# Heads of a bidirectional gated linear attention layer: log-decay sums moved to the first stage, states carried by VectorE with two factors in one operation, sums of squares written by ScalarE

## The chip, the core and the metric

The kernel runs on one core of one Trainium2 chip. Five engines work side by side, each through its own list of instructions in order: TensorE (PE, its weight loads PEld), VectorE (DVE), ScalarE (ACT), GpSimd (POOL) and SyncE (SP), which issues most of the DMA transfers. An instruction whose input is not ready holds up everything behind it on its engine. The metric is the device time of one launch in microseconds (us).

## The reference

One layer with two attention branches over a sequence of T = 1024 positions and a width of 1024. GLA has 4 heads (keys of 128, values of 256), HGRN 8 heads (keys of 128, values of 128). Each head runs a gated linear attention forwards and backwards in chunks of 64:

```
p = x @ W_in
g = log_sigmoid(low_rank(p)) / 16                       # GLA: log decay, <= 0
g = log(lb + (1 - lb) * sigmoid(p_f)),  k = 1 - exp(g)  # HGRN
b = cumsum(g) within a chunk of 64
o = (q * exp(b)) @ S  +  scores(q, k, exp(b_i - b_j)) @ v
S = exp(b_last) * S + (k * exp(b_last - b))^T @ v
o = forward + backward;  o * rsqrt(mean(o*o) + 1e-6) * gain * silu(gate);  then @ W_branch
y = sigmoid(m_a) * y_gla + sigmoid(m_h) * y_hgrn;  out = layer_norm(alpha * x + y @ W_out)
```

## The kernel before

**Three stages.** `dense` (0 to some 715 us of the profiled execution) makes all projections of x; every float32 product is done as three products of float32 numbers split into a high and a low part (`split`, L91 on ACT and L92 on DVE), with seven products in place of eight (`seven`). `heads` (about 715 to 1213 us) does the attention of the 12 heads and, between them, products that do not depend on them (`merge_gate`, later `gla_branch`; tile `proj`, L1364). The last stage (`hgrn_branch`, `final`) merges the branches, multiplies by W_out and normalises. Between stages everything passes through DRAM tensors: `logs` holds the log decays, `ks`, `qs`, `vd` and `gated` keys, queries, values and gates.

**Order.** The order on each engine is made by the framework's scheduler, which places instructions when the program is built, by priorities (raised in `high_priority` blocks) and by its own costs. On the chip the lists are fixed. A tile name has a fixed number of buffers; a new tile takes a buffer when the last reader of the old one is done.

**Log decays in `dense`.** `narrow_job` of kind decay (8 jobs, two directions of one HGRN head each) makes four 128x512 tiles `h`, from which POOL makes the keys (L1200) and ACT, in place, the logarithm (L1202); POOL's queue stores them to `logs`. `gla_logs` (8 calls, one for a head and a direction) works in two of five `raw` buffers of 128x1024, `f` and `m`: Abs, Exp and Ln on ACT (L1168 to L1171), the minimum and the difference on DVE (L1169, L1172), then a store. The same five `raw` buffers take the weights that are loaded for the next products.

**A head in `heads`.** `decays` loads the log decays into FB and FF. `scaled` sums them on DVE with a scan along 1024 columns that starts anew every 64 (L1422; `runs` is 1, and 0 at the starts), into PB and PF. It takes the ends of the halves (`logs`, `ends`), subtracts the middle (L1437), makes exp(-b) and exp(b) on ACT (L1440, L1441) and multiplies by keys and queries on DVE (L1443, L1442). `scores` makes the masked scores A (PE L382; DVE L392, L393, L395); `transposed` turns the keys (PE L540, ACT L541). PSUM tiles `sc`, `st`, `po` and `proj` have two buffers each.

**The states** (`states`) run once backwards (into Sb) and once forwards (into Sf), 7 steps each, over chunks of 128 positions. PE makes the products `st` (4 chunks in one PSUM tile for HGRN, 2 for GLA). ACT multiplies each by the decay of the near half into V (L1566), DVE adds the old state times the decay of the whole chunk (L1568, `tot`), and ACT multiplies by the decay of the next chunk's far half into Sb or Sf (L1572), which PE reads in the product `po` (L566).

**The norm** in `attend`: ACT squares a `po` tile of 128x512 (L1525), DVE adds up in groups of dv columns (L1526) and scales (L1528), POOL takes the power -1/2 (L1529), DVE multiplies by it and by the gate (L1533). PE transposes the result (L1540), ACT multiplies by the gain (`ot`, L1546), SP stores it to `oa` or `oh`. `gla_rows` loads `oa` back for the GLA branch product (tile `x`).

Of the kernel before, what the change touches and what calls it, by code (L numbers as in the profile page):

```python
# [12 lines left out]
AF = mybir.ActivationFunctionType  # L13
ALU = mybir.AluOpType
AX = mybir.AxisListType

P = 128
# [3 lines left out]
NT = T // P  # L21
# [853 lines left out]
class Fast(Layer):  # L875
# [283 lines left out]
    def gla_logs(self, h, d):  # L1159

        nc = self.nc
        f, m = self.t("raw"), self.t("raw")
        bias = self.prm[:, 4 * d + h : 4 * d + h + 1]
        for n in range(2):
            o = slice(512 * n, 512 * n + 512)
            ps = self.bank()
            nc.tensor.matmul(ps, self.ups[:, d, P * h : P * h + P], self.lr[:, o], start=True, stop=True)
            nc.scalar.activation(f[:, o], ps, AF.Abs, bias=bias)  # L1168
            nc.vector.tensor_scalar(out=m[:, o], in0=ps, scalar1=bias, scalar2=0.0, op0=ALU.add, op1=ALU.min)  # L1169
        nc.scalar.activation(f, f, AF.Exp, scale=-1.0)  # L1170
        nc.scalar.activation(f, f, AF.Ln, bias=1.0)  # L1171
        nc.vector.tensor_tensor(out=f, in0=m, in1=f, op=ALU.subtract)  # L1172
        self.store(self.logs[2 * h + d], f)

    def narrow_job(self, kind, at, w):
        nc = self.nc
        late = []

        def out(i, j, _, c, psum):
            s = c if kind == "copy" and not psum else self.h()  # L1180
            col = slice(512 * j, 512 * j + 512)
            if kind == "scale":
                nc.scalar.mul(s, c, QSCALE)
            elif kind != "copy":
                nc.scalar.activation(s, c, AF.Sigmoid)
            elif psum:
                nc.scalar.copy(s, c)
            if kind == "swish":
                nc.vector.scalar_tensor_tensor(out=s, in0=c, scalar=QSCALE, in1=s, op0=ALU.mult, op1=ALU.mult)
            if kind == "decay":  # L1190
                late.append((i, col, s))
            else:
                self.store((self.ks if kind == "copy" else self.qs)[at + i][:, col], s)

        self.seven(self.narrow_product(w, self.xs), 1, out, at == 0 and kind == "decay")
        for i, col, s in late:
            n = HGRN_HEADS * i + at
            o, b = self.omlb[:, n : n + 1], self.lb[:, n : n + 1]
            k = self.h()
            nc.gpsimd.tensor_scalar(out=k, in0=s, scalar1=self.nomlb[:, n : n + 1], scalar2=o, op0=ALU.mult, op1=ALU.add)  # L1200
            self.store(self.ks[GLA_HEADS + n][:, col], k)
            nc.scalar.activation(s, s, AF.Ln, scale=o, bias=b)  # L1202
            self.store(self.logs[2 * (GLA_HEADS + at) + i][:, col], s)

    def wide_job(self, kind, columns, w):
# [18 lines left out]
    def dense(self):  # L1224
        nc = self.nc
        self.slot, self.stage_one = T, True
        self.counts = {"raw": 5, "s": 3, "w": 8, "h": 14}
        heads = GLA_HEADS + HGRN_HEADS
        self.qs = self.dr.tile([heads, P, T], F32, name="qs")
        self.ks = self.dr.tile([GLA_HEADS + 2 * HGRN_HEADS, P, T], F32, name="ks")  # L1230
# [164 lines left out]

    def decays(self, n):

        fs = []
        for d in (1, 0):
            f = self.t("FB" if d else "FF")  # L1400
            self.nc.sync.dma_start(out=f, in_=self.logs[2 * n + d])
            fs.insert(0, f)
        return fs

    def key(self, n):
        k = self.t("K")
# [5 lines left out]
        self.nc.sync.dma_start(out=q, in_=self.qs[n])  # L1412
        return q

    def scaled(self, q, k, f, unit, d, index):

        nc = self.nc
        pr = self.t("PB" if d else "PF")
        last = 0 if d else 63
        seg = lambda a: a.rearrange("p (s j) -> p s j", j=64)  # L1420
        step = -1 if d else 1
        nc.vector.tensor_tensor_scan(  # L1422
            out=pr[:, ::step],
            data0=self.runs,
            data1=f[:, ::step],
            initial=0.0,
            op0=ALU.mult,
            op1=ALU.add,
        )
        logs = self.t(f"logs{d}", (P, NT, 2))  # L1430
        ends = self.t(f"ends{d}", (P, NT, 2))
        flat = lambda a: a.rearrange("p c h -> p (c h)")
        nc.vector.tensor_copy(out=flat(logs), in_=seg(pr)[:, :, last])
        nc.vector.tensor_reduce(out=self.minp[:, index : index + 1], in_=flat(logs), axis=AX.X, op=ALU.min)
        nc.scalar.activation(flat(ends), flat(logs), AF.Exp, scale=unit)
        half = pr.rearrange("p (c h j) -> p c h j", h=2, j=64)[:, :, d, :]
        nc.vector.tensor_tensor(  # L1437
            out=half, in0=half, in1=logs[:, :, d].unsqueeze(2).to_broadcast([P, NT, 64]), op=ALU.subtract
        )
        nc.scalar.activation(f, pr, AF.Exp, scale=-unit)  # L1440
        nc.scalar.activation(pr, pr, AF.Exp, scale=unit)  # L1441
        nc.vector.tensor_tensor(out=pr, in0=pr, in1=q, op=ALU.mult)  # L1442
        nc.vector.tensor_tensor(out=f, in0=f, in1=k, op=ALU.mult)  # L1443
        return pr, f, ends
# [26 lines left out]
    def heads(self):  # L1471
        nc = self.nc
        self.oa = self.dr.tile([KC, P, T], F32, name="oa")
        self.oh = self.dr.tile([KC, P, T], F32, name="oh")
        self.ua = self.dr.tile([KC, P, T], F32, name="ua")
        self.runs = self.t("runs")
        nc.vector.memset(self.runs, 1.0)
        nc.vector.memset(self.runs.rearrange("p (s j) -> p s j", j=64)[:, :, 0], 0.0)
        for n, name in enumerate(self.SEQUENCE):
            (self.gla_front if name[0] == "A" else self.hgrn_front)(int(name[1]))  # L1480
            if n == 0:
                self.plain_x()
            if n in (6, 8):
                self.gla_rows((n - 6) // 2)
            for i in self.MERGES[n]:
                self.merge_gate(i)
            if n >= 8:
                for i in (2 * n, 2 * n + 1):
                    self.gla_branch(i - 16)

    def attend(self, head, prepared, v, ve, dv, gate, gains, row):
        nc = self.nc
# [4 lines left out]
        per = 512 // dv  # L1497
# [11 lines left out]
        ss = self.t("ss", (P, NT), bufs=2)  # L1509
        rs = self.t("rs", (P, NT), bufs=2)  # L1510
        for g in range(NT // per):
            next(chain, None)
            po = self.att_ps("po")
            for j in range(per):
                c = per * g + j
                s = slice(P * c, P * c + P)
# [5 lines left out]
                self.product(po[:, dv * j : dv * j + dv], terms)  # L1522
            cs = slice(per * g, per * g + per)
            sq = self.t("sq", (P, 512))
            nc.scalar.activation(sq, po, AF.Square)  # L1525
            nc.vector.tensor_reduce(out=ss[:, cs], in_=sq.rearrange("p (c e) -> p c e", e=dv), axis=AX.X, op=ALU.add)  # L1526
            ms = self.msall[:, NT * head + per * g : NT * head + per * g + per]
            nc.vector.tensor_scalar(out=ms, in0=ss[:, cs], scalar1=1.0 / dv, scalar2=RMS_EPS, op0=ALU.mult, op1=ALU.add)  # L1528
            nc.gpsimd.tensor_tensor(out=rs[:, cs], in0=ms, in1=self.mhalf[:, cs], op=ALU.pow)  # L1529
            for j in range(per):  # L1530
                c = per * g + j
                gt = gate[:, c, ve : ve + dv]
                nc.vector.scalar_tensor_tensor(  # L1533
                    out=gt, in0=po[:, dv * j : dv * j + dv], scalar=rs[:, c : c + 1], in1=gt, op0=ALU.mult, op1=ALU.mult
                )
# [12 lines left out]

    def states(self, order, kt, v, ve, dv, ends, out_of, way):

        nc = self.nc
        per = 512 // dv
        near, far = (1, 0) if way == 1 else (0, 1)
        tot = self.t(f"tot{way}", (P, NT), bufs=2)
        nc.vector.tensor_tensor(out=tot, in0=ends[:, :, 0], in1=ends[:, :, 1], op=ALU.mult)
        order = list(order)
        state = None
        for b in range(0, len(order), per):
            pu = self.att_ps("st")
            batch = order[b : b + per]  # L1560
            us = [pu[:, dv * i : dv * i + dv] for i in range(len(batch))]
            for u, c in zip(us, batch):
                self.product(u, [(kt[:, P * c : P * c + P], v[:, c, ve : ve + dv])])
            for n, (u, c) in enumerate(zip(us, batch), b):
                new = self.t("V", (P, 256), bufs=6)[:, 0:dv]
                nc.scalar.mul(new, u, ends[:, c, near : near + 1])  # L1566
                if n:
                    nc.vector.scalar_tensor_tensor(  # L1568
                        out=new, in0=state, scalar=tot[:, c : c + 1], in1=new, op0=ALU.mult, op1=ALU.add
                    )  # L1570
                state = new
                nc.scalar.mul(out_of(n, c), state, ends[:, c + way, far : far + 1])  # L1572
            yield

    def judge(self):
# [116 lines left out]
    def run(self):  # L1692
        of = lambda *names: [f"{name}{k}" for name in names for k in range(4)]
        with ExitStack() as ctx:
# [3 lines left out]
            with ExitStack() as kept:  # L1698
                self.keep_x = self.pool(kept, "keepx")
                with ExitStack() as c:  # L1700
                    self.tops = self.pool(c, "tops")
                    self.stage(c, "p0", [["raw"], ["s"], ["w"], ["h"]])
                    self.dense()
                with ExitStack() as c:
                    self.stage(
# [6 lines left out]
                            ["Sf", "sq"],  # L1712
                            ["V"],
                            ["FB", "FF"],
                            ["runs"],
                            ["PB", "PF"],
                            ["v"],
                            ["A", "KT", "Sb"],
# [92 lines left out]
```

## Time and profile before

| | us |
|---|---|
| median of 3 runs | 1425.37 (1425.27 to 1426.08) |
| the profiled execution | 1426.49 |
| its span, from the first to the last record | 1424.80 |
| granted TensorE clock, mean of the span | 0.975 |

[...]

### The profile page before, as it was taken

The numbers are of one execution on the slowest core, as the hardware profiler recorded it, in microseconds if no ns is written. First come the engines' busy times: TensorE is split into PE (matmuls) and PEld (weight loads), VectorE is DVE, ScalarE is ACT, GpSimd is POOL, SyncE is SP. The second block draws the span as 40 slices with busy tenths as digits, with TensorE's granted clock in tenths as the row PEclk, the third lists the DMA queues.
The fourth block names the chain that finished last, engine by engine and source line by source line (L and its number), as shares of the span: only waits on it lengthen the run. The fifth ranks groups of instructions, "written<-read, shape, count | busy, mean of one in ns | idle before, by whom it ended". The sixth has DMA issues, their size and how long they took to land.

```text
span 1424.8 us, 21066 instructions
## 1 busy us (share of the span) xinstructions
PE 1339.6 (94%) x8009; PEld 1152.1 (81%) x8009; DVE 862.4 (61%) x1410; ACT 670.6 (47%) x1190; POOL 182.9 (13%) x270
## 2 busy tenths in 40 slices
PE   7999979999999999999989999987889999799996
PEld 5888858877799999999968877765677888577885
DVE  8755645776566665544463666766788443665544
ACT  6656565774533333222244565556676454653100
POOL 1234350111111011011100010111110100000011
PEclk9999989999999999999999999998899999899998
DMA  7444342333433332332473454355565331865431
GB/s 274 140 148 167 129 151 101 135 138 111 154 131 108 107 102 99 99 114 104 144 278 121 139 185 166 109 177 177 178 231 212 104 112 60 294 231 169 150 103 55
DMA packets 83153, 210.45 MB, mean 148 GB/s; under 512 B 10656, under 2 KB 10656, under 8 KB 80992
## 3 DMA queue, kind: packets, MB, share of 16 engines
q1 hardware_dynamic: 68368, 160.48, 33.1%
q0 software_dynamic: 14672, 48.51, 9.0%
q8 instruction: 65, 1.06, 0.3%
q14 instruction: 48, 0.39, 0.1%
HBM read 137.65 MB, written 71.30 MB: 147 GB/s over the span
## 4 chain that ended last, share of the span: by engine, by line
PE 71%; DMA 10%; DVE 7%; ACT 5%; issue 5%; POOL 0%; SPq 0%; DVEq 0%; POOLq 0%; ACTq 0%
PE bank L988 22%; PE bank L975 16%; PE proj L1364 12%; PE bank L1636 6%; PE po L566 4%; PE st L566 3%; DMA raw<-in_dram 3%; PE sc L382 2%; DMA wraw<-in_dram 2%; PE bank L1304 2%; DMA g<-ua 2%; DMA oa<-ot 1%; PE sc L540 1%; DVE PF L1422 1%; DMA hraw<-oa 1%
## 5 line engine op out<-in xcount | busy, mean ns | idle before, releaser
L975 PE MATMUL bank<-xP,w 128*128 128x512 f32 x1344 | 315.5, 395 | 13.6 <-DVE h L1012 7.0
L988 PEld LDWEIGHTS bank<-w,xP 128*128 128x128 f32 x2688 | 323.5, 192 | 1.1 <-DVE w L92 0.8
L988 PE MATMUL bank<-w,xP 128*128 128x256 f32 x2688 | 323.6, 283 | 0.3 <-DVE w L92 0.3
L975 PEld LDWEIGHTS bank<-xP,w 128*128 128x128 f32 x1344 | 255.1, 190 | 71.4 <-DVE h L1012 8.4
L1364 PE MATMUL proj<-x,hw 128*128 128x512 f32 x576 | 147.1, 399 | 0.1
L92 DVE TENSOR_TENSOR w<-s,w 128x512 fp32r<-128x512 f32 (+1 forms) x96 | 84.0, 877 | 76.3 <-ACT w L91 76.1
L91 ACT CAST w<-s 128x512 fp32r<-128x512 f32 (+1 forms) x96 | 72.6, 760 | 121.7 <-PE bank L988 78.7
L91 ACT CAST w<-raw 128x512 fp32r<-128x512 f32 (+1 forms) x90 | 65.1, 732 | 128.4 <-PE bank L988 67.0
L1364 PEld LDWEIGHTS proj<-x,hw 128*128 128x128 f32 x576 | 104.9, 188 | 21.9 <-issue 0.7
L1364 PE MATMUL proj<-xP,hw 128*128 128x512 f32 x360 | 97.8, 411 | 6.3 <-DVE hw L92 5.5
L1364 PE MATMUL bank<-oh,hw 128*128 128x512 f32 x384 | 93.1, 401 | 9.9 <-ACT hw L91 4.8
L1529 POOL TENSOR_TENSOR rs<-msall,mhalf 128x4 f32<-128x4 f32 (+1 forms) x32 | 43.0, 1343 | 447.2 <-DVE msall L1528 444.5
L1364 PEld LDWEIGHTS bank<-oh,hw 128*128 128x128 f32 x384 | 72.4, 192 | 30.5 <-ACT hw L91 7.9
L1012 DVE TENSOR_TENSOR h<-bank,h 128x512 f32<-128x512 f32 x96 | 65.8, 687 | 45.9 <-PE bank L988 33.4
L92 DVE TENSOR_TENSOR w<-raw,w 128x512 fp32r<-128x512 f32 (+1 forms) x90 | 75.3, 843 | 29.6 <-ACT w L91 29.6
L1364 PEld LDWEIGHTS proj<-xP,hw 128*128 128x128 f32 x360 | 67.2, 193 | 21.9 <-DVE hw L92 6.6
L1012 DVE TENSOR_TENSOR h<-h,bank 128x512 f32<-128x512 f32 x65 | 44.4, 684 | 53.9 <-PE bank L988 28.7
L92 DVE TENSOR_TENSOR hw<-hraw,hw 128x512 fp32r<-128x512 f32 x64 | 43.8, 687 | 42.5 <-ACT hw L91 42.5
L1566 ACT ACTIVATE V<-st,ends 128x128 f32<-128x128 f32 (+1 forms) x168 | 58.6, 414 | 22.5 <-PE st L566 22.2
L566 PE MATMUL st<-v,KT 128*128 128x128 f32 (+1 forms) x336 | 61.0, 323 | 2.6 <-ACT KT L541 1.4
L1304 PE MATMUL bank<-xP,w 128*128 128x512 f32 x216 | 52.3, 404 | 8.0 <-ACT xP L91 6.6
L91 ACT CAST hw<-hraw 128x512 fp32r<-128x512 f32 x64 | 39.6, 618 | 36.9 <-PE proj L1364 25.6
(194 smaller groups left out, 2008.2 us busy)
## 6 DMA issues: line engine op xcount, KB each, us to landing
raw<-in_dram SPq DMA_DIRECT2D x82, 256.0 KB, 3.2
hraw<-in_dram SPq DMA_DIRECT2D x68, 256.0 KB, 3.5
raw<-in_dram SPq DMA_DIRECT2D x33, 512.0 KB, 3.7
ks<-h POOLq DMA_DIRECT2D x40, 256.0 KB, 3.1
K<-ks SPq DMA_DIRECT2D x20, 512.0 KB, 4.9
logs<-h POOLq DMA_DIRECT2D x32, 256.0 KB, 3.7
gated<-h POOLq DMA_DIRECT2D x32, 256.0 KB, 2.7
vd<-h POOLq DMA_DIRECT2D x32, 256.0 KB, 2.7
```

The costliest lines, as they stand in the source:

```text
L91: nc.scalar.copy(hi, raw)
L92: (lo_engine or nc.gpsimd).tensor_tensor(out=lo, in0=raw, in1=hi.bitcast(F32), op=ALU.subtract)
L382: mm = lambda out, l, r: nc.tensor.matmul(out, l, r, start=True, stop=True)
L566: self.nc.tensor.matmul(out, l, r, start=(i == 0), stop=(i == len(terms) - 1))
L975: self.nc.tensor.matmul(out[0], a[i][:, k, :], b[k][:, j, :], start=(n == 0 and not more), stop=(n == len(terms) - 1), skip_group_check=True,)
L988: self.nc.tensor.matmul(out[c // 2][:, 256 * (c % 2) : 256 * (c % 2) + 256], b[k][:, j, P * c : P * c + P], a[i][:, k, :], start=(n == 0 a ...
L1012: nc.vector.tensor_tensor(out=to[n], in0=one[n], in1=two[n], op=op)
L1304: self.nc.tensor.matmul(ps, w.both[a][:, k, :], xs[k][:, b, :], start=(m == 0), stop=(m == len(terms) - 1))
L1364: nc.tensor.matmul(ps, parts[k][a], self.plain[k, n][:, b, :], start=(m == 0), stop=(m == len(terms) - 1))
L1529: nc.gpsimd.tensor_tensor(out=rs[:, cs], in0=ms, in1=self.mhalf[:, cs], op=ALU.pow)
L1566: nc.scalar.mul(new, u, ends[:, c, near : near + 1])
L1636: nc.tensor.matmul(pss[m], y[:, k, rows], self.wo[k, n][:, j, part], start=(i == 0), stop=(i == len(terms) - 1))
```

## The change

Four things change.

- **Sums in `dense`.** The scan moves from `scaled` to `sum_up`, which runs in place on a log-decay tile before it is stored, in pieces of 512 columns with `runs` of that width. There are 32 pieces in the decay jobs and 16 in `gla_logs`. To make room for `runs`, `h` has 13 buffers and no longer 14. In `heads` the loads of `logs` go into PB and PF, and FB and FF are only written by ACT. In GLA the store of `f` and in HGRN that of `h` now wait for DVE.
- **States by DVE.** Both multiplications of a step become one DVE operation with two factors (`tensor_scalar`), and the sum with the old state comes before it: `total = entered + u`, `entered = total * near * far`. ACT's 336 multiplications and `tot` go. The products `st` stay in PSUM until DVE's chain has come to them.
- **Sums of squares.** ACT squares in pieces of dv columns (96 in all) with an accumulator output for the sum; the 32 reductions on DVE go.
- **Buffers.** `runs` leaves the second stage.

```diff
         nc.vector.tensor_tensor(out=f, in0=m, in1=f, op=ALU.subtract)
+        self.sum_up(f, d)
         self.store(self.logs[2 * h + d], f)
+
+    def sum_up(self, f, d):
+
+        for n in range(f.shape[1] // 512):
+            u = f[:, 512 * n : 512 * n + 512][:, :: -1 if d else 1]
+            self.nc.vector.tensor_tensor_scan(out=u, data0=self.runs, data1=u, initial=0.0, op0=ALU.mult, op1=ALU.add)
...
             nc.scalar.activation(s, s, AF.Ln, scale=o, bias=b)
+            self.sum_up(s, i)
             self.store(self.logs[2 * (GLA_HEADS + at) + i][:, col], s)
...
-        self.counts = {"raw": 5, "s": 3, "w": 8, "h": 14}
+        self.runs = self.t("runs", (P, 512))
+        nc.vector.memset(self.runs, 1.0)
+        nc.vector.memset(self.runs.rearrange("p (s j) -> p s j", j=64)[:, :, 0], 0.0)
+        self.counts = {"raw": 5, "s": 3, "w": 8, "h": 13}
...
-            f = self.t("FB" if d else "FF")
-            self.nc.sync.dma_start(out=f, in_=self.logs[2 * n + d])
+            pr = self.t("PB" if d else "PF")
+            self.nc.sync.dma_start(out=pr, in_=self.logs[2 * n + d])
...
-        pr = self.t("PB" if d else "PF")
+        f = self.t("FB" if d else "FF")
...
-        nc.vector.tensor_tensor_scan(
...
-            nc.scalar.activation(sq, po, AF.Square)
-            nc.vector.tensor_reduce(out=ss[:, cs], in_=sq.rearrange("p (c e) -> p c e", e=dv), axis=AX.X, op=ALU.add)
+            for j in range(per):
+                o, c = slice(dv * j, dv * j + dv), per * g + j
+                nc.scalar.activation(sq[:, o], po[:, o], AF.Square, accum_out=ss[:, c : c + 1])
...
-                new = self.t("V", (P, 256), bufs=6)[:, 0:dv]
-                nc.scalar.mul(new, u, ends[:, c, near : near + 1])
                 if n:
-                    nc.vector.scalar_tensor_tensor(
-                        out=new, in0=state, scalar=tot[:, c : c + 1], in1=new, op0=ALU.mult, op1=ALU.add
-                    )
-                state = new
-                nc.scalar.mul(out_of(n, c), state, ends[:, c + way, far : far + 1])
+                    total = self.t("V", (P, 256), bufs=6)[:, 0:dv]
+                    nc.vector.tensor_tensor(out=total, in0=entered, in1=u, op=ALU.add)
+                    u = total
+                entered = out_of(n, c)
+                nc.vector.tensor_scalar(
+                    out=entered,
+                    in0=u,
+                    scalar1=ends[:, c, near : near + 1],
+                    scalar2=ends[:, c + way, far : far + 1],
+                    op0=ALU.mult,
+                    op1=ALU.mult,
+                )
```

What this does to the lists of instructions is shown at three places. In the rows a number behind x counts equal instructions in a row; a scan is printed as SCALAR_TENSOR_TENSOR with `runs` among its inputs; lines of the changed kernel are numbered by its own text.

DVE in `dense`, in the second of the decay jobs: `w` are split weights of the next job, `s` their sums, L1012 adds a product from PSUM (`bank`) into `h`.

```order
@@ -108,4 +114,5 @@
 L92 TENSOR_TENSOR w<-raw,w 128x512
 L1012 TENSOR_TENSOR h<-bank,h 128x512
+L1180 SCALAR_TENSOR_TENSOR h<-runs,h 128x512 x4
 L92 TENSOR_TENSOR w<-s,w 128x512
 L953 TENSOR_TENSOR s<-raw,s 128x512
```

The four scans of a job stand in one piece, ahead of the next split.

DVE in `heads`, the forward states of HGRN head 2 and what follows them, before:

```order
L1568 SCALAR_TENSOR_TENSOR V<-V,tot_9135 128x128 x3
L392 TENSOR_TENSOR A<-sc,m_70 128x512
L1568 SCALAR_TENSOR_TENSOR V<-V,tot_9135 128x128 x3
L92 TENSOR_TENSOR x<-hraw,x 128x512
L1526 TENSOR_REDUCE ss<-sq 128x4
L92 TENSOR_TENSOR hw<-hraw,hw 128x512
L1422 SCALAR_TENSOR_TENSOR PB<-runs,FB 128x1024
L1528 TENSOR_SCALAR msall<-ss 128x4
L1422 SCALAR_TENSOR_TENSOR PF<-runs,FF 128x1024
L393 TENSOR_TENSOR sq<-sc,m_71 128x256
```

And in the changed kernel, the last steps of the same states:

```order
L1569 TENSOR_SCALAR Sf<-V,ends_8924 128x128
L1566 TENSOR_TENSOR V<-Sf,st 128x128
L1569 TENSOR_SCALAR Sf<-V,ends_8924 128x128
L1566 TENSOR_TENSOR V<-Sf,st 128x128
L392 TENSOR_TENSOR A<-sc,m_70 128x512
L1569 TENSOR_SCALAR Sf<-V,ends_8924 128x128
L92 TENSOR_TENSOR x<-hraw,x 128x512
L1528 TENSOR_SCALAR msall<-ss 128x4
L92 TENSOR_TENSOR hw<-hraw,hw 128x512
L393 TENSOR_TENSOR sq<-sc,m_71 128x256
```

The two scans ahead of L393 are gone, and each step of the states is two DVE operations that depend on each other.

PE in the last head, from the end of the transposes of its keys (L540) to the second product with Sf, before:

```order
L540 MATMUL sc<-ident,FF 128x128 x4
L1364 MATMUL proj<-x,hw 128x512 x20
L566 MATMUL st<-v,KT 128x128 x7
L566 MATMUL po<-Sb,PB 128x128 x2
L566 MATMUL po<-v,A 128x128
L566 MATMUL po<-Sb,PB 128x128
L1364 MATMUL proj<-x,hw 128x512 x16
L566 MATMUL po<-Sf,PF 128x128
```

And in the changed kernel:

```order
L540 MATMUL sc<-ident,FF 128x128 x6
L1375 MATMUL proj<-x,hw 128x512 x23
L566 MATMUL po<-Sb,PB 128x128
L566 MATMUL st<-v,KT 128x128 x4
L1375 MATMUL proj<-x,hw 128x512 x2
L566 MATMUL st<-v,KT 128x128
L566 MATMUL po<-Sb,PB 128x128
L566 MATMUL po<-v,A 128x128
L566 MATMUL po<-Sb,PB 128x128
L566 MATMUL st<-v,KT 128x128 x2
L1375 MATMUL proj<-x,hw 128x512 x8
L566 MATMUL po<-Sf,PF 128x128
```

The forward products `st` are cut into 4, 1 and 2, with other work of PE between them.

## Rows read from the trace of the kernel before

**Rows 1.** The page, part 1: busy us of each engine, share and instructions.

```profile
PE 1339.6 (94%) x8009; PEld 1152.1 (81%) x8009; DVE 862.4 (61%) x1410; ACT 670.6 (47%) x1190; POOL 182.9 (13%) x270
```

**Rows 2.** Stretches in heads: length, busy us (instructions) by engine, PEclk, DMA, GB/s.

```profile
720.00:740.00 20.00, 14.78 (x53) 11.39 (x52) 17.05 (x28) 9.79 (x16) 1.08 (x2) 0.83 0.63 229
940.00:1080.00 140.00, 112.13 (x759) 92.63 (x759) 106.32 (x213) 88.89 (x201) 18.00 (x12) 0.90 0.55 191
1100.00:1200.00 100.00, 99.57 (x635) 84.55 (x636) 46.62 (x100) 46.41 (x111) 6.41 (x4) 1.00 0.31 106
715.00:1213.00 498.00, 462.49 (x2909) 378.86 (x2908) 318.19 (x626) 279.73 (x626) 42.57 (x33) 0.97 0.45 159
```

**Rows 3.** Timeline of PE in heads: start, us, what, [idle before <-releaser].

```profile
733.62 5.41 PE L1364 MATMUL proj<-xP,hw 128*128 128x512 f32 x12 [4.37 <-DVE hw L92]
959.23 1.11 PE L540 MATMUL sc<-ident,FB 128*128 128x128 f32 x4 [4.01 <-DVE sq L393]
986.15 1.19 PE L566 MATMUL po<-v,A 128*128 128x256 f32 x2 [4.13 <-DVE msall L1528]
1015.06 0.62 PE L566 MATMUL po<-v,A 128*128 128x128 f32 x2 [1.60 <-ACT ot L1546]
1028.32 0.24 PE L382 MATMUL sc<-PB,FB 128*64 128x64 f32 x1 [1.82 <-DVE sq L393]
```

**Rows 4.** Chain that ended last, 954 to 960 us: start, us, what.

```profile
954.48 2.05 issue
956.67 2.19 DVE PF L1422
958.86 0.31 DVE sq L393
```

**Rows 5.** DVE groups in heads: xcount | busy us, mean ns | idle before, releasers.

```profile
L1422 DVE TENSOR_TENSOR_SCAN PB<-runs,FB 128x1024 f32<-128x1024 f32 x12 | 27.4, 2283 | 1.4 <-PE po L566 1.2
L1568 DVE SCALAR_TENSOR_TENSOR V<-V,tot 128x128 f32<-128x128 f32 x48 | 16.8, 351 | 23.7 <-ACT V L1566 20.4
L1533 DVE SCALAR_TENSOR_TENSOR gate<-po,rs,gate 128x128 f32<-128x128 f32 x56 | 15.7, 341 | 0.2 <-POOL rs L1529 0.2
L1533 DVE SCALAR_TENSOR_TENSOR gate<-po,rs,gate 128x256 f32<-128x256 f32 x32 | 13.9, 476 | 2.0 <-POOL rs L1529 1.9
L1526 DVE TENSOR_REDUCE ss<-sq 128x2 f32<-128x512 f32 x16 | 10.9, 682 | 18.4 <-ACT sq L1525 18.2
L393 DVE TENSOR_TENSOR sq<-sc,m 128x256 f32<-128x256 f32 x24 | 9.8, 410 | 0.0
```

**Rows 6.** Timeline of DVE: three steps of one state chain.

```profile
1007.43 1.19 DVE L1568 SCALAR_TENSOR_TENSOR V<-V,tot-1_9082 128x128 f32<-128x128 f32 x3
```

**Rows 7.** ACT groups in heads, and DVE's waits for ACT (us, times, longest).

```profile
L1566 ACT ACTIVATE V<-st,ends 128x128 f32<-128x128 f32 (+1 forms) x168 | 58.6, 414 | 22.5 <-PE st L566 22.2
L1572 ACT ACTIVATE Sb<-V,ends 128x128 f32<-128x128 f32 (+1 forms) x84 | 34.2, 468 | 0.6 <-DVE V L1568 0.4
L1572 ACT ACTIVATE Sf<-V,ends 128x128 f32<-128x128 f32 (+1 forms) x84 | 33.0, 453 | 13.2 <-PE po L566 11.9 <-DVE V L1568 1.1
L1525 ACT ACTIVATE sq<-po 128x512 f32<-128x512 f32 x30 | 17.9, 598 | 30.1 <-PE po L566 30.0
DVE V L1568 <- ACT V L1566: 58.3, 35, 6.6
```

**Rows 8.** Stretches of the first stage; columns as in rows 2.

```profile
100.00:180.00 80.00, 80.00 (x354) 66.24 (x354) 45.14 (x66) 47.13 (x70) 29.46 (x45) 1.00 0.42 145
280.00:300.00 20.00, 19.93 (x88) 16.16 (x87) 15.79 (x25) 13.94 (x20) 2.40 (x6) 1.00 0.37 132
```

**Rows 9.** Timeline of PE among the calls of gla_logs.

```profile
316.19 4.16 PE L975 MATMUL bank<-xP,w 128*128 128x512 f32 x17 [1.22 <-DVE w L92]
388.08 5.49 PE L975 MATMUL bank<-xP,w 128*128 128x512 f32 x12 [2.98 <-DVE h L1012]
```

**Rows 10.** DMA issues: count, KB each, median us to landing.

```profile
FB<-logs SPq DMA_DIRECT2D x12, 512.0 KB, 4.0
```

More of the change, by code (lines that the diff above doesn't have):

```diff
@@ L1396, in decays @@
     def decays(self, n):
-        fs = []
+        sums = []
         for d in (1, 0):
-            f = self.t("FB" if d else "FF")
-            self.nc.sync.dma_start(out=f, in_=self.logs[2 * n + d])
-            fs.insert(0, f)
-        return fs
+            pr = self.t("PB" if d else "PF")
+            self.nc.sync.dma_start(out=pr, in_=self.logs[2 * n + d])
+            sums.insert(0, pr)
+        return sums
     def key(self, n):
@@ L1413, in query, with scaled @@
         return q
-    def scaled(self, q, k, f, unit, d, index):
+    def scaled(self, q, k, pr, unit, d, index):
         nc = self.nc
-        pr = self.t("PB" if d else "PF")
+        f = self.t("FB" if d else "FF")
         last = 0 if d else 63
         seg = lambda a: a.rearrange("p (s j) -> p s j", j=64)
-        step = -1 if d else 1
-        nc.vector.tensor_tensor_scan(
[L1423 to L1428, printed above, removed]
-        )
         logs = self.t(f"logs{d}", (P, NT, 2))
@@ L1475, in heads @@
         self.ua = self.dr.tile([KC, P, T], F32, name="ua")
-        self.runs = self.t("runs")
-        nc.vector.memset(self.runs, 1.0)
-        nc.vector.memset(self.runs.rearrange("p (s j) -> p s j", j=64)[:, :, 0], 0.0)
         for n, name in enumerate(self.SEQUENCE):
@@ L1553, in states @@
         near, far = (1, 0) if way == 1 else (0, 1)
-        tot = self.t(f"tot{way}", (P, NT), bufs=2)
-        nc.vector.tensor_tensor(out=tot, in0=ends[:, :, 0], in1=ends[:, :, 1], op=ALU.mult)
         order = list(order)
-        state = None
+        entered = None
         for b in range(0, len(order), per):
@@ L1564, in states @@
             for n, (u, c) in enumerate(zip(us, batch), b):
-                new = self.t("V", (P, 256), bufs=6)[:, 0:dv]
-                nc.scalar.mul(new, u, ends[:, c, near : near + 1])
                 if n:
-                    nc.vector.scalar_tensor_tensor(
-                        out=new, in0=state, scalar=tot[:, c : c + 1], in1=new, op0=ALU.mult, op1=ALU.add
-                    )
-                state = new
-                nc.scalar.mul(out_of(n, c), state, ends[:, c + way, far : far + 1])
+                    total = self.t("V", (P, 256), bufs=6)[:, 0:dv]
[10 more added lines that the diff above has]
+                )
             yield
@@ L1701, in run @@
                     self.tops = self.pool(c, "tops")
-                    self.stage(c, "p0", [["raw"], ["s"], ["w"], ["h"]])
+                    self.stage(c, "p0", [["runs"], ["raw"], ["s"], ["w"], ["h"]])
                     self.dense()
@@ L1714, in run @@
                             ["FB", "FF"],
-                            ["runs"],
                             ["PB", "PF"],
```

## The prediction

> **What bounds the kernel now.** I read the busy times first: PE has 94% of the span, DVE 61%, ACT 47% [rows 1]. So only time that PE loses can be won. The table of stretches shows where that is. From 1100 to 1200 us PE loses nothing, at clock 1.00. From 940 to 1080 us it is idle for 140 - 112.1 = 27.9 us and has a granted clock of 0.90, which is another 0.10 x 140 = 14 us at most, since part of it falls on the idle time. At the start of the heads, 720 to 740 us, it is idle for 5.2 us. The heads as a whole leave PE idle for 498 - 462.5 = 35.5 us, and their clock is 0.97 [rows 2].
>
> Third, the timeline of PE says what ended those waits [rows 3]. At 733.6 PE waited 4.37 us for a split on DVE, at 959.2 for 4.01 us and at 1028.3 for 1.82 us for L393 (4.01 us once more, at 997.7, in the same pattern). Last, the chain of waits shows what DVE did then: a piece of 2.05 us without a named cause, the scan into PF for 2.19, and only then L393 [rows 4]. The unnamed piece is the first scan of the pair, since a scan lasts 2.28 us [rows 5] and the two stand together in DVE's list. Two scans thus hold up short operations that PE needs.
>
> **What the change takes away in the heads.** DVE loses 24 scans of 2.28 us, 54.8 us; 32 reductions of 0.68, 21.8; and 144 additions of the states, 96 at 0.351 and 48 at some 0.48 (L1533 at 256 columns has 0.476), 56.7 [rows 5]. With `tot`, a few us, that is some 137 us. ACT loses 58.6 + 34.2 + 33.0 = 125.8 us of multiplications and 32 squares of 0.598, 19.1 [rows 7].
>
> **What it adds in the heads.** DVE gets 144 sums of a product in PSUM with the last state. L393 has such a form, 0.410 at 256 columns; from there to 128 I take off the 0.135 that lies between the two forms of L1533: 0.275 [rows 5]. 96 x 0.275 + 48 x 0.410 = 46 us. The 168 operations with two factors are in no row of this trace. The nearest is L1533, with one factor and two tensors: 0.341 and 0.476. That is my value, 112 x 0.341 + 56 x 0.476 = 65 us. The lower end is the part of L1533 that doesn't grow with the columns, 0.341 - 0.135 = 0.206, which gives 35 us; the upper end I put at 80, a quarter more than my value.
>
> Each step now depends on the one before inside DVE. Three dependent steps took 1.19 us [rows 6], so one starts 0.42 after the last, 0.07 more than its length: 312 x 0.07 = 22 us. Sum 133 added against 137 taken: DVE's load in the heads hardly changes. What changes is its grain, since no block of 4.4 us is left.
>
> [...]
>
> [...]
>
> ACT gets 96 squares of 128 or 256 columns with a sum. From below they cost what the 32 large ones did (19 us), from above 96 times the mean of L1566, 0.414, or 40 us [rows 7]; writing the sum isn't shown, and I bound it by 0 and once more 40 us. I take 40 together. ACT is still relieved by some 105 us.
>
> **The state chain.** A step was 0.42 us on DVE for HGRN, with ACT before and behind; it becomes 0.275 + 0.341 + 2 x 0.07 = 0.76. Seven steps (the first has no sum) take 4.9 us, against 6 x 0.42 and two ACT operations of about 0.4, 3.3 us. For GLA it is 6.7 against some 4.3. Two chains a head: 8 x 3.2 + 4 x 4.8 = 45 us of longer latency in all. On the other side DVE's 58.3 us of waits for ACT's multiplications go [rows 7]. PE's list covers most of the rest: between the last backward `st` and the first `po<-Sb` of the last head stand 23 matmuls at 0.228, 5.2 us, against a chain of 4.9. I charge 3 us of the 45 as open.
>
> **The first stage.** 48 scans of 512 columns: half of 2.28 is 1.14, and half the fixed 0.206 on top makes 1.24; together 60 us. They hide or not by place. From 100 to 180 us, in the decay jobs, DVE is busy for 45 of 80 us and PE never idle [rows 8]. Four scans for each job, at four such jobs in the stretch, add 20 us: 65 of 80, still free. The block of four, 5 us, stands where DVE mostly waited for ACT's logarithms. Cost 0 to 1 us a job.
>
> Among the calls of `gla_logs` it is tighter: from 280 to 300 us DVE is busy for 15.8 of 20 us [rows 8], and two scans, 2.5 us, come with each of the 8 calls. PE waits there already, 1.22 us for a split and 2.98 us for an addition on DVE [rows 9]. The tile `f` also keeps its `raw` buffer longer, and the next weights are loaded into such a buffer. If every call cost PE its 2.5 us, it would be 20 us; if none did, 0. I take 4, because PE is idle there in places only. One buffer fewer for `h` I put at nothing: a decay job takes 11, so one is reused a little over a job later.
>
> **Loads.** PB and PF must be free before their load starts, as they had to be before the scan; then 4.0 us of DMA [rows 10] replaces 4.6 us of DVE. No change in latency, but DVE is free meanwhile.
>
> **The sum**, against 1426.5 us of the profiled execution, 1.1 above the median:
> - start of the heads, four scans ahead of the split that PE awaits: -4 of the 4.37 [rows 3];
> - scan pairs ahead of PE's work, 940 to 1080 us: of 27.9 us idle some 15 ended at DVE operations behind scans (4.01 twice, 1.82 and smaller ones up to 1070). Two thirds: -10. The rest meets the next late thing: L1528 at the end of a chain of stores and loads, 4.13 us at 986, or `ot`, 1.60 at 1015 [rows 3];
> - clock: PE falls to the low level behind its idle time; half of the 14 us comes back: -6;
> - ACT relieved, so that transposed keys and `ot` come earlier: -6, a sixth of the heads' idle time;
> - state chain +3, first stage +4.
>
> That is -19: 1407.5 profiled, 1406 as a median.
>
> **The rivals.**
> - *Much faster.* The heads keep PE as full as from 1100 to 1200 us: of 35.5 idle and 14 of clock 45 come back, +3 +4 stay: -38, 1387 us. For it: the scans explain half, and ACT had 89 of 140 us there. Against: waits for stores and loads of `oa` stay. Chance 0.16.
> - *The load takes the scan's place.* If the load into PF, which now waits for the `po` of two heads before, ends as late as the scan did, the -10 and most of the clock stay out: -4 -6 +3 +4 = -3, 1422 us. Against: at 959 PE waited for another head's L393, not for the sum itself. Chance 0.08.
> - *The first stage gives it back.* Each of the 8 calls costs PE its whole 2.5 us: 20 in place of 4, so -3, and with 1 us for some decay jobs 1425. For it: 15.8 + 2.5 of 20 us. Against: the stretch as a whole isn't that dense. Chance 0.08.
> - *Slower: the longer chain becomes PE's wait.* Place: `po<-Sb` and `po<-Sf` behind DVE, and `st`, whose PSUM tile now stays taken until the chain has passed. Without the chain the sum is -22, so it decides from half of the 45 us on. With three quarters, 34 us: +12, 1437. For it: PE's 27.9 us of idle time from 940 to 1080 show that it has little else to do there [rows 2], and the chain shares DVE with all else. Against: those stretches were waiting for ACT. Chance 0.12.
>
> **Chances and range.** My forecast has 0.56, between 1394 and 1418. A difference under 0.2%, 2.9 us, can't be told from none. Faster: 0.56 + 0.16 and half of the load's case, 0.76. The same: the other half, and most of the first stage's case, 0.10. Slower: 0.14. For eight in ten the range goes from 1388, which cuts the lower half of the first rival, to 1429, which cuts the last one.
>
> **What would show it.** Right: in the heads no scan, L393 and the splits without waits of 4 us, PE idle by some 15 us less, clock over 0.97, ACT down by 100 us; in the first stage 48 scans of 1.2 us and PE idle by about 4 us more between 270 and 390 us. Wrong: PE's waits named `po<-Sf` or `st` behind DVE's L1566 or L1569 with more than 20 us in all; or waits for `w` and `h` in the first stage that grow by 15 us; or the two-factor operation over 0.6 us.

## The result and the profile after

The kernel after takes 1411.44 us (median of 4 runs, 1410.43 to 1413.81), the one before 1425.72 in the same session: a ratio of 0.9892, with a 95% interval of 0.9861 to 0.9922. The forecast was 1406 us, in a range from 1388 to 1429. The profiled run of after took 1410.43 us with a span of 1408.6, 16.2 less than before.

The page of after, part 1, against [rows 1]: ACT has 93.6 us less, DVE 34.3 more, and PE 12.5 us less for the same 8009 matmuls.

```profile
PE 1327.1 (94%) x8009; PEld 1145.2 (81%) x8009; DVE 896.7 (64%) x1546; ACT 577.0 (41%) x1014; POOL 172.3 (12%) x270
```

The stretches of before, cut at 720 us and just behind the heads (length, busy us and instructions by engine, PEclk as a share of full speed, DMA, GB/s):

```profile
0.00:720.00 720.00, 696.12 (x4273) 626.29 (x4274) 423.60 (x578) 331.62 (x464) 125.75 (x220) 0.99 0.39 135
720.00:1222.00 502.00, 462.63 (x2921) 378.71 (x2919) 322.64 (x642) 281.16 (x629) 44.05 (x34) 0.96 0.46 159
1222.00:1424.80 202.80, 180.80 (x816) 147.13 (x816) 116.18 (x190) 57.79 (x98) 13.10 (x16) 0.95 0.48 164
```

The same of after, with two stretches that answer to [rows 2]:

```profile
0.00:720.00 720.00, 693.14 (x4277) 623.59 (x4278) 476.76 (x626) 331.40 (x464) 129.68 (x220) 0.99 0.39 135
720.00:1206.00 486.00, 454.91 (x2918) 374.74 (x2916) 304.80 (x733) 189.03 (x454) 29.34 (x34) 0.97 0.47 162
1206.00:1408.60 202.60, 179.02 (x816) 146.88 (x816) 115.11 (x188) 56.55 (x96) 13.26 (x16) 0.95 0.50 170
720.00:740.00 20.00, 19.30 (x85) 15.40 (x83) 7.31 (x19) 8.00 (x16) 1.08 (x2) 1.00 0.68 254
940.00:1080.00 140.00, 115.58 (x808) 95.86 (x807) 103.02 (x255) 60.90 (x154) 10.66 (x12) 0.90 0.59 205
```

All of the gain lies in the heads: 502 us became 486. There PE's idle time fell from 39.4 to 31.1 us (8.3), of which 4.5 at the start (5.2 to 0.7 between 720 and 740 us), and its busy time by 7.7 us, for nearly as many matmuls at a granted clock of 0.97 in place of 0.96 (at the start, between 720 and 740 us, 1.00 in place of 0.83). The first stage did 53 us more of DVE work in the same time: its idle time on PE grew by 3.0 us and its busy time fell by as much, and the heads' first matmul came at 727.18 us (728.06 before). Between 940 and 1080 us PE still idles for 24.4 us and the clock is 0.90 as it was.

What PE waited for there now, on its timeline (start, us, what, [idle before <-releaser]), against [rows 3]:

```profile
727.18 0.73 PE L1375 MATMUL proj<-xP,hw 128*128 128x512 f32 x2 [0.70 <-ACT hw L91]
958.41 1.22 PE L566 MATMUL st<-v,KT 128*128 128x256 f32 x2 [3.33 <-DVE V L1566]
989.82 0.79 PE L566 MATMUL po<-v,A 128*128 128x128 f32 x2 [4.25 <-ACT ot L1546]
```

The 0.70 us at 727 were 0.85 before. The waits of 4 us for splits and for L393 are gone, and two of 3 and 4 us have come. DVE's timeline of after shows what held V:

```profile
949.10 0.41 DVE L1569 TENSOR_SCALAR Sb<-V,ends 128x256 f32<-128x256 f32 x1
949.43 1.22 DVE L1445 TENSOR_TENSOR FB<-FB,K 128x1024 f32<-128x1024 f32 x1
952.38 0.17 DVE L1435 COPY logs<-PF 128x16 f32<-128x16 f32 x1 [1.74 <-DMA PF<-logs]
952.47 0.41 DVE L1566 TENSOR_TENSOR V<-Sb,st 128x256 f32<-128x256 f32 x1
...
957.33 0.69 DVE L92 TENSOR_TENSOR x<-hraw,x 128x512 fp32r<-128x512 f32 x1 [2.31 <-ACT x L91]
957.94 0.41 DVE L1566 TENSOR_TENSOR V<-Sb,st 128x256 f32<-128x256 f32 x1
```

One step of the state chain stands behind a copy that waits for a load (1.74 us), the next behind a split that waits for ACT (2.31). The two operations of a step take 0.8 us together, so this wait doesn't come from the chain's own length: the chain shares DVE's list with work that waits, and the PSUM tile of `st` stays taken until its last step.

ACT's timeline of after shows what held `ot`:

```profile
984.17 0.69 ACT L1546 ACTIVATE ot<-po,prm 128x512 f32<-128x512 f32 x1
984.75 1.06 ACT L1443 ACTIVATE PB<-PB 128x1024 f32<-128x1024 f32 x1
989.08 0.69 ACT L1546 ACTIVATE ot<-po,prm 128x512 f32<-128x512 f32 x1 [3.27 <-DMA oa<-ot]
```

ACT stood still for 3.27 us with its whole list behind it, because the third `ot` needs the buffer of the first, whose store was under way. The chain that ended last has that store (start, us, what):

```profile
980.06 8.94 DMA oa<-ot
989.42 3.48 DMA oa<-ot
993.01 0.69 ACT ot L1546
```

### The profile page after: what moved, and what is told of

Same layout as the page of the kernel before. It is cut to its first block, busy times and chain, and to the rows that moved or that the text cites. A ratio compares the mean times of both kernels' runs of the same rounds, so it can differ in the third digit from the quotient of the medians.

```text
span 1408.6 us, 20930 instructions
## 1 busy us (share of the span) xinstructions
PE 1327.1 (94%) x8009; PEld 1145.2 (81%) x8009; DVE 896.7 (64%) x1546; ACT 577.0 (41%) x1014; POOL 172.3 (12%) x270
## 4 chain that ended last, share of the span: by engine, by line
PE 72%; DMA 12%; DVE 5%; ACT 5%; issue 4%; POOL 1%; SPq 0%; POOLq 0%; DVEq 0%; ACTq 0%
PE bank L988 22%; PE bank L975 15%; PE proj L1375 14%; PE bank L1640 6%; PE po L566 5%; PE st L566 3%; PE sc L382 3%; DMA raw<-in_dram 2%; PE bank L1315 2%; DMA g<-sigs 2%; DMA hraw<-oa 2%; DMA g<-ua 2%; DMA oa<-ot 1%; DMA hraw<-in_dram 1%; PE sc L540 1%
## 5 line engine op out<-in xcount | busy, mean ns | idle before, releaser
L1375 PE MATMUL bank<-oh,hw 128*128 128x512 f32 x384 | 91.3, 397 | 12.5 <-ACT hw L91 9.6
L1012 DVE TENSOR_TENSOR h<-bank,h 128x512 f32<-128x512 f32 x96 | 65.7, 686 | 41.8 <-PE bank L988 34.7
L1529 POOL TENSOR_TENSOR rs<-msall,mhalf 128x4 f32<-128x4 f32 (+1 forms) x32 | 28.3, 883 | 445.9 <-DVE msall L1528 445.9
L1012 DVE TENSOR_TENSOR h<-h,bank 128x512 f32<-128x512 f32 x65 | 44.5, 685 | 53.2 <-PE bank L988 30.0
L1526 ACT ACTIVATE sq<-po 128x128 f32<-128x128 f32 (+1 forms) x96 | 28.8, 311 | 110.9 <-PE po L566 110.9
```

What stands on the lines that cost most here:

```text
L1012: nc.vector.tensor_tensor(out=to[n], in0=one[n], in1=two[n], op=op)
L1375: nc.tensor.matmul(ps, parts[k][a], self.plain[k, n][:, b, :], start=(m == 0), stop=(m == len(terms) - 1))
L1526: nc.scalar.activation(sq[:, o], po[:, o], AF.Square, accum_out=ss[:, c : c + 1])
```

## Experiments

All times are ratios to the kernel before, measured in the same session (its median there 1427.5 to 1428.2 us), with 95% intervals. 0.001 is 1.4 us. The kernels are scheduled anew after every edit, so each ratio holds the edit and the reordering that it brings; no run kept the order fixed.

### One part alone

**Sums in the first stage only.**

```diff
+            self.sum_up(s, i)
             self.store(self.logs[2 * (GLA_HEADS + at) + i][:, col], s)
...
-        nc.vector.tensor_tensor_scan(
-            out=pr[:, ::step],
```

> The kernel before with one part of the change: the sums of log decays are made in the first stage, states and squares stay as they were. Theory 1 (the scans' grain: short operations that PE needs stood behind pairs of 2.28 us): most of the gain of 14 to 16 us is here, the 4.4 us at the start of the heads and the waits behind L393 between 940 and 1080 us; 1412 to 1415 us. Theory 2 (ACT relieved of the states' multiplications is what counts): only the start of the heads is gained, 1421 to 1423 us. By both, the first matmul of the heads comes within 1 us of where it was.

Measured: 0.9874 (0.9848 to 0.9901), 18 us. Theory 1 holds, with a little more than it said: this part alone gives the whole gain.

**States on VectorE only.**

```diff
-                new = self.t("V", (P, 256), bufs=6)[:, 0:dv]
-                nc.scalar.mul(new, u, ends[:, c, near : near + 1])
+                    nc.vector.tensor_tensor(out=total, in0=entered, in1=u, op=ALU.add)
```

> The kernel before with one part of the change: the states are carried by VectorE alone, scans and squares stay where they were. Theory 1 (the scans' grain): a chain on DVE that now stands behind scan pairs at every step gains nothing, 1424 to 1431 us, with PE waits behind V and Sf. Theory 2 (ACT relieved): 10 us or more are gained here, 1412 to 1416 us.

Measured: 1.0019 (1.0005 to 1.0033), slower by some 3 us, though ACT's busy time fell from 670.6 to 567.1. Theory 2 is out.

**Squares only.**

```diff
-            nc.scalar.activation(sq, po, AF.Square)
-            nc.vector.tensor_reduce(out=ss[:, cs], ...
+                nc.scalar.activation(sq[:, o], po[:, o], AF.Square, accum_out=ss[:, c : c + 1])
```

> The kernel before with one part of the change: sums of squares come out of ScalarE. Theory 1: 21.8 us of reductions leave DVE, which also stood ahead of what PE needs, against 19.6 us of reads of the sums on a fuller ACT; 1422 to 1425 us. Rival (ACT, which still has the multiplications, becomes late with copies and transposed keys): 1427 to 1432 us. By theory 2 it is slower too, by 1 to 3 us, since ACT gets more to do.

Measured: 0.9947 (0.9928 to 0.9966), 7.6 us faster: more than theory 1 said, and ACT, 13.7 us fuller, did not become late.

What a part does to PE shows in the table of PE's waits between 715 and 1200 us (us in total, times, longest). Before:

```profile
PE sc L540 <- DVE sq L393: 8.0, 2, 4.0
PE po L566 <- DVE msall L1528: 5.8, 2, 4.1
PE proj L1364 <- DVE hw L92: 5.5, 3, 4.4
```

With the states on VectorE only, those for L393 and the split stay:

```profile
PE po L566 <- ACT ot L1546: 9.5, 3, 4.6
PE proj L1364 <- DVE hw L92: 7.9, 6, 4.6
PE sc L540 <- DVE sq L393: 7.3, 2, 3.7
```

With the sums moved only, L393 has no row left in that table, and its costliest rows are:

```profile
PE st L566 <- ACT V L1565: 6.4, 7, 1.6
PE proj L1375 <- ACT hw L91: 3.5, 3, 1.6
PE po L566 <- ACT ot L1545: 3.0, 4, 1.3
...
PE proj L1375 <- DVE hw L92: 1.4, 1, 1.4
```

Between 940 and 1080 us PE then idles for 21.8 us, where it was 27.9, and the clock is 0.94, where it was 0.90:

```profile
940.00:1080.00 140.00, 118.24 (x780) 95.44 (x778) 94.81 (x219) 93.93 (x212) 10.85 (x12) 0.94 0.61 209
```

With the squares only, 7.2 us behind L393 (in five waits, the longest 3.2) and 5.0 behind the split are left. So moving the scans ends these waits, and neither other part does it alone. Whether the length of a scan or the 54.8 us of load counts, no run separates: none kept the scans in the heads in shorter pieces, and the squares took away 21.8 us in pieces of 0.68 and gained 7.6.

### One part left out

The kernel after was timed again beside these three.

> The kernel after, unchanged, on the chip of the three runs that leave one part out, so that they are compared on equal terms. By the first measurement: 0.989 of the kernel before.

Measured: 0.9880 (0.9857 to 0.9904).

**Without the state part** (states as before).

```diff
-                    nc.vector.tensor_tensor(out=total, in0=entered, in1=u, op=ALU.add)
+                nc.scalar.mul(new, u, ends[:, c, near : near + 1])
```

> The kernel after with the states carried as before (ACT multiplies, VectorE adds); sums in the first stage and squares from ScalarE stay. Alone, sums gave a ratio of 0.987, states 1.002, squares 0.995, and all three 0.989. Theory A (sums and squares take away the same waits: reductions and scans both stood ahead of what PE needs on DVE, so the squares add nothing once the scans are gone): 0.986 to 0.990. Theory B (the state part costs, since its longer chain and its 30 us more of DVE take from what the others give): sums and squares add up, 0.982 to 0.985.

Measured: 0.9823 (0.9794 to 0.9852), faster than the kernel after by 0.0057, with an uncertainty of about 0.0037 (the root of the summed squares of both half widths). Theory B.

**Without the squares** (one square of 512 columns, reduction on DVE).

```diff
-                nc.scalar.activation(sq[:, o], po[:, o], AF.Square, accum_out=ss[:, c : c + 1])
+            nc.scalar.activation(sq, po, AF.Square)
```

> The kernel after with the squares made as before (one square of 512 columns on ACT, a reduction on DVE); sums and states stay. Theory A: as the kernel after, 0.987 to 0.990, since the squares add nothing. Theory B (the states cost): worse than the sums alone (0.987) by what the states cost, 0.990 to 0.994, since the reductions of 0.68 us stand in DVE's list between the steps of its longer state chain.

Measured: 0.9886 (0.9864 to 0.9908), as the kernel after: here theory A is nearer. PE's waits for V on DVE were 9.9 us there, 3.3 in the kernel after.

**Without the sums** (scans in the heads).

```diff
-            self.sum_up(s, i)
...
+        nc.vector.tensor_tensor_scan(
+            out=pr[:, ::step],
```

> The kernel after with the sums of log decays made in the heads as before; states and squares stay. Both theories: the scans' waits stay, the wait of 4.4 us at the start of the heads and the ones behind L393; squares give 0.995 and states cost 0.002: 0.996 to 1.000, about 1421 us. If the forecast's term for the relief of ACT (6 us) were right, it would be 0.990 to 0.993.

Measured: 0.9950 (0.9934 to 0.9966), just below the range of both theories; not the 0.990 to 0.993 by which ACT's relief would have shown. Of the waits that were to stay, only the one at the start did (4.2 us for the split). In the profiled execution L393 holds PE for 0.9 us in all, though the scans still stand ahead of it; PE waits instead for L1534, the multiplication by the gate, which now stands beside the scans:

```profile
PE po L1541 <- DVE gate L1534: 7.0, 3, 2.6
PE sc L540 <- DVE sq L393: 0.9, 2, 0.6
```

A part of the scans' price thus shows under the name of another operation that stands behind them.

The eight combinations of the three parts:

| parts made | ratio |
|---|---|
| none | 1 |
| states | 1.0019 |
| squares | 0.9947 |
| squares, states | 0.9950 |
| sums | 0.9874 |
| sums, states | 0.9886 |
| sums, squares | 0.9823 |
| all | 0.9880 and 0.9892 |

Sums give 0.012 to 0.013 in three of the four pairs and 0.007 in the last, squares 0.005 to 0.007 in three and nothing in the last. The states never gain: +0.002, 0.000, +0.001, and +0.006 where the other two are made; only the first and the last of these are clear of their uncertainty. Why they cost most there is not settled; the interval allows from 0.002 to 0.009.

### The loop through ot

```diff
-"V": 6, "ot": 2,
+"V": 6, "ot": 4,
```

> The kernel after with four buffers of the output tile ot in place of two. Theory (what was late next is the loop ot, store to oa, load of hraw from oa, with ACT waiting at its head): PE's waits for ot (4.25, 1.90 and 1.43 us between 950 and 1000 us) go or shrink, 1405 to 1408 us. Rival (the stores' own latency of 8 us sets it, or the chain of states does; buffers change nothing): 1410 to 1413 us.

Measured: 0.9825 (0.9801 to 0.9850), against 0.9880 and 0.9892 for the kernel after, which had its runs in other sessions. ACT's wait for `oa<-ot`, 5.4 us between 900 and 1080, has no row left. The gain is there, more than the theory said (1401.7 us), but the traces don't show that this wait is its cause. In the second profiled execution of the kernel after (that of the repeated measurement, 1411.0 us) ACT waits for `oa<-ot` for 0.9 us in place of 5.4, and PE for `ot` for 6.1 us in place of 9.9, and the kernel takes no less time for it; with four buffers PE still waits for `ot` for 5.3 us. The new order that came with the buffers is a rival that no run tests.

**Four buffers, states as before.**

```diff
-                    nc.vector.tensor_tensor(out=total, in0=entered, in1=u, op=ALU.add)
+                nc.scalar.mul(new, u, ends[:, c, near : near + 1])
...
-"V": 6, "ot": 2,
+"V": 6, "ot": 4,
```

> Sums in the first stage and squares from ScalarE, states as before, and four buffers for ot in place of two. The two-buffer version of it had a ratio of 0.982, and four buffers took 0.006 off the kernel after. If PE's waits for ot are what is left in both: 0.975 to 0.979. If the two cures are for one wait (ACT, with more to do here, sets ot by itself): 0.980 to 0.984.

Measured: 0.9799 (0.9774 to 0.9823). Against 0.9823 with two buffers the intervals overlap, so this pair doesn't decide.

### Scans made twice in the first stage

```diff
+            zeros = self.runs[:, 0:1].to_broadcast([P, 512])
+            self.nc.vector.tensor_tensor_scan(out=u, data0=zeros, data1=u, initial=0.0, op0=ALU.mult, op1=ALU.add)
             self.nc.vector.tensor_tensor_scan(out=u, data0=self.runs, data1=u, initial=0.0, op0=ALU.mult, op1=ALU.add)
```

> The kernel after with each scan of the first stage preceded by one of the same shape that changes nothing (its factors are all zero, so each element is its own sum): 48 x 1.208 = 58 us more on DVE there. In the kernel after the first matmul of the heads stood at 727.2 us (728.1 before), so the first 48 scans cost nothing in place of the 4 us forecast. Theory (DVE's free time in the first stage covers them): the second 48 cost 0 to 3 us as well, the first matmul of the heads comes at 727 to 730 us. Rival (the free time among the gla_logs calls was used up by the first): 16 scans of 1.2 us show on PE there, 10 to 19 us, a ratio of 0.995 to 1.003.

Measured: 0.9990 (0.9975 to 1.0005), some 15 us slower than the kernel after. In the profiled execution the heads' first matmul comes at 751.2 us, 24 later, and the span is 19.4 us longer, so a part of the 24 is won back behind it. The rival holds, but at another place than it said: the first `bank` of `low_product` (L1143) starts at 226.5 us against 210.4, so 16 of the 24 us are lost in the decay jobs. DVE's timeline and then PE's, with the scans doubled (L1181 and L1182):

```profile
190.02 0.67 DVE L92 TENSOR_TENSOR w<-raw,w 128x512 fp32r<-128x512 f32 x1
190.60 1.22 DVE L1181 TENSOR_TENSOR_SCAN h<-runs,h 128x512 f32<-128x512 f32 x1
191.74 1.20 DVE L1182 TENSOR_TENSOR_SCAN h<-runs,h 128x512 f32<-128x512 f32 x1
192.85 1.20 DVE L1181 TENSOR_TENSOR_SCAN h<-runs,h 128x512 f32<-128x512 f32 x1
193.97 0.67 DVE L92 TENSOR_TENSOR w<-s,w 128x512 fp32r<-128x512 f32 x1
194.55 2.33 DVE L1182 TENSOR_TENSOR_SCAN h<-runs,h 128x512 f32<-128x512 f32 x2
```

```profile
199.74 4.57 PE L975 MATMUL bank<-xP,w 128*128 128x512 f32 x12 [6.58 <-DVE h L1012]
```

The kernel after has a block of four scans of 4.57 us in that place, and a wait of 3.77 where before had 2.04: the free time was nearly used up by the first 48.

### A third way for the states

Both factors of a step are multiplied beforehand into `tot`; ACT takes the product from PSUM times that, VectorE adds the last state times the same.

```diff
-                    nc.vector.tensor_tensor(out=total, in0=entered, in1=u, op=ALU.add)
...
-                nc.vector.tensor_scalar(
+                    nc.scalar.mul(new, u, factor)
+                    nc.vector.scalar_tensor_tensor(out=to, in0=state, scalar=factor, in1=new, op0=ALU.mult, op1=ALU.add)
```

> The kernel after with the states done in a third way: both factors of a step are multiplied beforehand, ACT takes u from PSUM times their product, and one operation on VectorE adds the last state times the same product. A step is one operation on DVE (0.35 us) in place of two (0.29 + 0.35), and one on ACT in place of none; the PSUM tile is free once ACT has read it. Theory (the state part costs because its chain is two operations long on DVE and keeps the PSUM tile): PE's waits for st behind DVE's V go, 0.979 to 0.984, as without the state part or better. Rival (ACT's list, held at its head by loads of oa and stores of ot, is what is late): ACT gets 50 us back on its list, 0.987 to 0.990 as the kernel after.

Measured: 0.9770 (0.9747 to 0.9792), 1393.0 us. The theory holds, by more than it said; the rival is out, though ACT's busy time rose from 577.0 to 629.1. Against the kernel without the state part (0.9823, another session) DVE has the same load, 848.7 and 848.1 us, and ACT has 54 us less: what is gained there is the shorter chain, or this time the relief of ACT.

With four buffers:

```diff
-"V": 6, "ot": 2,
+"V": 6, "ot": 4,
```

> The same with four buffers for ot. If ot and the states are separate waits: 0.006 less than with two buffers, 0.973 to 0.979. If they are one: the same as with two.

Measured: 0.9704 (0.9680 to 0.9727), 1383.2 us: 42 us under the kernel before and some 25 under the change as made. By the ratios the two cures add up. Where the second one acts is not shown: in the two profiled executions the heads end alike, with the first `bank<-oh` of the last stage at 1191.7 us (two buffers) and 1191.1 (four). PE's costliest waits, of which the first stands at that border, and its groups of the states (xcount | busy us, mean ns | idle before):

```profile
PE bank L1375 <- ACT hw L91: 8.5, 1, 8.5
PE po L1540 <- DVE gate L1533: 6.2, 4, 4.2
PE po L566 <- DVE Sb L1574: 3.3, 1, 3.3
```

```profile
L1574 DVE SCALAR_TENSOR_TENSOR Sf<-Sf,tot,V 128x128 f32<-128x128 f32 x48 | 16.8, 350 | 18.7 <-ACT V L1573 15.2
L1573 ACT ACTIVATE V<-st,tot 128x128 f32<-128x128 f32 x48 | 14.0, 372 | 1.5 <-PE st L566 1.5
```

No wait for `st` behind DVE's V is left (2.6 us behind ACT's). This form has a chain of one operation, frees the PSUM tile from ACT, and takes 48 us off DVE (848.8 against 896.7); which of the three counts most, no run separates.

## Why the prediction was right in its sum and wrong in its split

The total fell by 14 us as a median and by 16 between the profiled executions, 19 forecast. That it came out so near is partly luck: one term had the wrong sign, and a part of the change that had no term made up for it.

**Start of the heads, -4:** right. The wait of 4.37 us is gone, PE's idle time between 720 and 740 us fell by 4.5; a wait of 1.2 us for a split on ACT, at 742.5, is new.

**Scan pairs, -10, and clock, -6:** the mechanism was right for the scans, the split was not. The run with the sums alone holds these two, the start and the first stage: -16 forecast, -18 (-22 to -14) measured. In the kernel after, PE's idle time behind 740 us fell by only 3.8 us, with what ACT and the chain contributed inside it, and its busy time in the heads by 7.7. The clock term failed in its place: between 940 and 1080 us, where the prediction had it, the clock stayed at 0.90, and it rose at the start of the heads, from 0.83 to 1.00, some 3 us of the 20. In before the clock is low around a long wait, 0.73 and 0.59 in the two pieces of 5 us from 955, with the 4.01 us for L393 in them, and 1.00 from 965 to 980; but not around all idle time: in the kernel after PE idles for 4.5 of the 10 us from 1050, and the clock is 1.00 there and in the next 10. Of the three parts alone the sums raised it between 940 and 1080 us to 0.94, which is 0.04 x 140 = 6 us, as forecast (0.88 with the states, 0.91 with the squares). The prediction said that the rest "meets the next late thing" and named `ot` at 1.60 us; in the kernel after, `ot` cost 9.9 us in six waits (6.1 in five in the other execution).

**ACT relieved, -6, and state chain, +3:** this step failed. Together -3 was forecast; the state part alone measured +3, and +8 beside the other two. ACT's list lost 93.6 us of work and its waits grew: for `hraw<-oa` from 8.0 to 25.5 us between 900 and 1080. Its list had less work and got no further: what it waited for came no earlier, as far as these waits show. On the other side the chain was priced by its latency, 45 us of which 3 would show, since PE's list would cover the rest with matmuls of 0.228 us: in the chain that ended last of before 46 of them took 10.47, at a granted clock of 1.00 (start, us, what).

```profile
1101.66 10.47 PE proj L1364 x46
```

The rows at 952 and 957 us show another price, steps that stand behind foreign waits in DVE's list.

**Squares:** they had no term of their own. Their 21.8 us of reductions went into "DVE's load in the heads hardly changes". Alone they gave -7.6 us and beside the sums -7 (0.9874 to 0.9823), about what the states then cost; beside sums and states both, nothing is left of it (0.9886 to 0.9880). That is how the failed step was covered.

**First stage, +4:** 0 measured, by 3.0 us more idle time against 3.0 less busy time. Of the idle time 1.7 us lie between 190 and 220 us and 0.4 between 270 and 390, where the prediction looked for all of it. The scans last 1.208 us, 1.24 forecast. The place was wrong: the danger lay in the decay jobs, which the prediction called free, and not among the `gla_logs` calls.

**Prices.** Groups of DVE and then of ACT in the heads:

```profile
L1180 DVE TENSOR_TENSOR_SCAN h<-runs,h 128x512 f32<-128x512 f32 x32 | 37.1, 1208 | 9.8 <-ACT h L1209 9.8
...
L1566 DVE TENSOR_TENSOR V<-Sb,st 128x128 f32<-128x128 f32 x48 | 13.7, 286 | 1.6
L1569 DVE TENSOR_SCALAR Sb<-V,ends 128x128 f32<-128x128 f32 x48 | 16.6, 345 | 1.4
L1569 DVE TENSOR_SCALAR Sb<-V,ends 128x256 f32<-128x256 f32 x24 | 9.8, 410 | 0.6
L1569 DVE TENSOR_SCALAR Sb<-st,ends 128x128 f32<-128x128 f32 x8 | 3.3, 409 | 9.7 <-PE st L566 9.7
L1569 DVE TENSOR_SCALAR Sb<-st,ends 128x256 f32<-128x256 f32 x4 | 2.2, 540 | 0.0
```

```profile
L1526 ACT ACTIVATION_READ_ACCUMULATOR sq<-po 128x1 f32 x96 | 19.6, 204 | 0.0
L1526 ACT ACTIVATE sq<-po 128x128 f32<-128x128 f32 x64 | 16.8, 277 | 58.4 <-PE po L566 58.4
```

(The scans' row is of the first stage.) The sums of a product with the last state cost 0.286 where 0.275 was taken, the 168 two-factor operations 64 us in all their groups where 65 was. DVE's busy time in the heads fell by 18 us and not by 4, since the forecast had counted 22 us of latency between the steps as load. Squares with their sums have 48.4 us of busy time, 40 forecast.

**The rivals.** The load in the scan's place took part (1.74 us at 952) without deciding. The slower case has its wait, 3.33 us for V, once, far from the 34 us that it needed. The much faster case, 1387 us, is what this change did not reach; the third way of doing the states came to 1393.0, and with four buffers to 1383.2.

## What to carry to other kernels

Long operations that stand ahead of short ones on a shared engine can go to a stage where that engine waits anyway (0.9874 with this part alone), but that stage's free time is spent once: the first 48 scans cost nothing, the next 48 some 15 us. Moving work off an engine need not gain anything: 94 us less on ACT went into waits, for loads of `oa` among others. For a recurrence over PSUM tiles, letting another engine scale the tile out of PSUM, with one dependent operation per step, was the best of the three forms here (0.9770, against 0.9823 for the form of before and 0.9880 for that of the change). A sum that fits says nothing of its terms: the runs with one part alone or left out did.

## What the runs showed of the hardware

In the rows of L1569 a two-factor `tensor_scalar` grows by 65 ns from 128 to 256 columns when it reads SBUF (345 to 410) and by 131 when it reads PSUM (409 to 540), with the same rest of 0.28 us. So in these rows reading PSUM costs more by the column, 64 ns at 128 columns and 130 at 256, and not by a fixed amount. Though columns from SBUF cost half as much, the operation was no cheaper than L1533 before (345 ns against 341), since its fixed rest is larger: 280 against 206.

A square with a sum comes as two instructions on ACT, and the second, which reads the sum out, took 204 ns as a mean of 96, against 277 for the square of 128 columns itself. The two overlap, so busy time overstates what they hold ACT: of these squares with 256 columns, 0.38 and 0.20 us long with the read, the second starts 0.37 us behind the first (ACT's timeline in the kernel after: start, us, what).

```profile
978.03 0.38 ACT L1526 ACTIVATE sq<-po 128x256 f32<-128x256 f32 x1 [1.32 <-PE po L566]
978.31 0.20 ACT L1526 ACTIVATION_READ_ACCUMULATOR sq<-po 128x1 f32 x1
978.40 0.38 ACT L1526 ACTIVATE sq<-po 128x256 f32<-128x256 f32 x1
```
